# Stick-breaking attention: transposes by query tile into a step buffer, a float32 value product one step later, and one elementwise product on GpSimd

## The chip, the cores and the metric

The kernel runs on one core of a Trainium2 chip. The metric is device time in microseconds (us) of one execution; lower is better. The kernel before has a median of 3163.7 us over three runs.

The engines are called as in the profile: PE (matrix products; PEld is its weight load), DVE (VectorE), ACT (ScalarE), POOL (GpSimd) and SP (which issues nearly all DMAs).

## What is computed

One layer of a hybrid block over 2048 tokens of width 1024, all in float32. The part that the change touches is branch B, stick-breaking attention with 16 heads of 64 values, strictly causal:

```python
logits = einsum('bqhd,bkhd->bhqk', q, k) * 64 ** -0.5
log_fail = where(ki < qi, log_sigmoid(-logits), 0)
between = cumsum(log_fail, axis=3, reverse=True) - log_fail
w = where(ki < qi, exp(log_sigmoid(logits) + between), 0)
out = einsum('bhqk,bkhd->bqhd', w, v)
```

So the weight of a key is its sigmoid ("stick weight") times the product, over all later keys up to the query, of one minus theirs ("running product"). Around it stand an RMS norm, one large input projection, a Mamba-2 scan (branch A, 16 heads), gates, two branch projections and an output projection.

## The kernel before

Activations are kept with features on the partitions. Large products run in the type `float32r`, with both operands split in a high and a low half, so that one product of 128 x 128 x 512 is three PE instructions (`product`, L139). The stages follow each other: norm and transposes of the input, the first projections, V (`prep_v`, `unit_v`, L389 to L423), the scan of branch A with its projections (`ssd`, up to L640), attention with the rest of the projections as fill, and the final projections.

V is made by 16 units per group of four heads. A unit sums 24 products into `vps`; ACT rounds the result to its high half, DVE subtracts to get the low half (L421, L422), and SP stores both, side by side, to `vst` in memory.

Attention works in 160 steps `(h, qs, kc)`: for each head, query blocks `qs` of 512 from the last to the first, and for each of them key blocks `kc` of 512 from the diagonal back to the first. So each head has ten steps, four of them diagonal (`kc == qs`) and six full. A query block has four query tiles `i` of 128.

- `attn_load` (from L809) loads Q, K and V of a step two steps ahead.
- `attn_qk(s, i)` (from L829) makes the logits of one query tile in two PE products, `lg`. ACT makes both sigmoids, `tc` (of the negative, L843) and `sw` (the stick weight, L845). On diagonal steps POOL masks both with a select (L847, L849) and only the columns up to the diagonal are used. DVE runs the running product along the keys, from the end (L852), with the carry of the later key block as start; DVE multiplies `sw` by it (L853); POOL copies the carry `cy` for the next key block (L856). POOL also sets the one start column of `tc` (L842).
- `attn_tr(s, kb)` (from L862) transposes on PE, for one key tile `kb`, the blocks of all four query tiles into `wtp`; ACT rounds them to `wh` (L870) and DVE subtracts to get `wl` (L872).
- `attn_av(s, kb)` (from L875) adds two products to `po`: stationary is V with its high and low halves, 128 columns, moving are `wh` and then `wl`. At the last key block ACT and DVE add the two halves of `po` and gate them with `zl` (L886 to L893).

The order of PE is fixed: a helper chains every PE instruction to the one traced before it. The other engines get their instructions from a scheduler that mostly follows the traced order. In one step, query tile by query tile, PE does the transposes of key tile `i`, the logits of the next step's tile `i`, the value product of key tile `i - 2`, and some fill; after the four tiles come the last two value products and fill. The fill is a stream of 34 x 96 projection products for nine tenths of the steps, and 192 products of the first output projection for the last head; `FW` (L27) sets the share of each of the six fill places of a step.

Of the kernel before, what the change touches and what calls it, by code (L numbers as in the profile page):

```python
# [18 lines left out]
P = 128  # L19
# [4 lines left out]
HD = 64  # L24
EPS = 1e-6
WARM = 24
FW = (0.8, 0.9, 1.0, 1.0, 1.1, 1.2)  # L27

COL_Z = 0
COL_X = 1024  # L30
# [18 lines left out]
def hybrid_kernel(ctx, tc, x, norm_pre, w_in, b_gate, conv_w, conv_b, dt_bias, a_log, d_skip,  # L49
# [57 lines left out]

    kst = [drp.tile([P, L], F32, name=f"kst{h}") for h in range(HEADS)]
    qst = [drp.tile([P, L], F32, name=f"qst{h}") for h in range(HEADS)]
    vst = [drp.tile([L, 4, P], F32, name=f"vst{i}") for i in range(HEADS // 4)]  # L110
    csd = drp.tile([HEADS, L], F32, name="csd")
    ytd = [drp.tile([D, TB], F32, name=f"ytd{t}") for t in range(NTB)]
    otd = [drp.tile([D, TB], F32, name=f"otd{t}") for t in range(NTB)]
# [272 lines left out]
    with tc.tile_pool(name="va", bufs=2) as va, tc.tile_pool(name="vp", bufs=2, space=PSUM) as vp:  # L386
        kn = va.tile([P, NCH, 16], F32, name="kn", bufs=1)

        def prep_v(i):  # L389
            c0, cw = vch[i]  # L390
            vh, vl = [], []
            for k in range(KT):
                raw = va.tile([P, cw], F32, name="vraw", tag="vraw", bufs=4)
                nc.sync.dma_start(raw, w_in[k * P:(k + 1) * P, c0:c0 + cw])
                h = va.tile([P, cw], F32R, name="vhi", tag="vhi", bufs=12)
                nc.scalar.copy(h, raw)
                l = va.tile([P, cw], F32R, name="vlo", tag="vlo", bufs=12)
                nc.vector.tensor_sub(l, raw, h.bitcast(F32))
                vh.append(h)
                vl.append(l)  # L400
            return vh, vl

        def unit_v(i, c, wv):
            c0, cw = vch[i]
            vh, vl = wv
            off = cw - VW
            tb, o = c // CPB, (c % CPB) * P
            ps = vp.tile([P, TB], F32, name="vps", tag="vps", bufs=3)
            for k in range(KT):
                xh, xl = hh[tb][:, k, o:o + P], hl[tb][:, k, o:o + P]  # L410
                matmul(ps[:, :cw], xh, vh[k], start=(k == 0), stop=False)
                yield
                matmul(ps[:, :cw], xh, vl[k], start=False, stop=False)
                yield
                matmul(ps[:, :cw], xl, vh[k], start=False, stop=(k == KT - 1))
                yield
            if off:
                nc.vector.tensor_copy(kn[:, c, :], ps[:, :16])
            v = va.tile([P, 4, 2, HD], F32R, name="vt", tag="vt", bufs=3)
            src = ps[:, off:cw].rearrange("p (h d) -> p h d", d=HD)  # L420
            nc.scalar.copy(v[:, :, 0, :], src)  # L421
            nc.vector.tensor_sub(v[:, :, 1, :], src, v[:, :, 0, :].bitcast(F32))  # L422
            nc.sync.dma_start(vst[i][c * P:(c + 1) * P], v.bitcast(F32).rearrange("p h s d -> p h (s d)"))  # L423

        def last_k():
            knf = kn.rearrange("p c d -> p (c d)")
            kd = kst[HEADS - 1].rearrange("(s d) t -> d s t", s=2)
            for r0 in range(0, NCH * 16, P):
                n = min(P, NCH * 16 - r0)
                tp = vp.tile([P, P], F32, name="ktp", tag="ktp")  # L430
                transpose(tp[:n], knf[:, r0:r0 + n], ident)
                kt = va.tile([P, 2, P], F32R, name="kt", tag="kt")
                nc.scalar.copy(kt[:n, 0, :], tp[:n])
                nc.vector.tensor_sub(kt[:n, 1, :], tp[:n], kt[:n, 0, :].bitcast(F32))
                for c in range(n // 16):
                    t0 = (r0 // 16 + c) * P
                    nc.sync.dma_start(kd[HD - 16:HD, :, t0:t0 + P], kt[c * 16:(c + 1) * 16].bitcast(F32))

        wv = prep_v(0)
        for tb in range(NTB):  # L440
            run(proj(w9, tb, done_qk(ev, 9, tb)))
        for i in range(len(vch)):
            for c in range(NCH):
                if c == max(0, NCH - 6) and i + 1 < len(vch):
                    nxt = prep_v(i + 1)
                run(unit_v(i, c, wv))
            if i == 0:
                later(20, last_k)
            if i + 1 < len(vch):
                wv = nxt  # L450
        wb = prep_a(COL_B)
        flush()
# [326 lines left out]

    steps = [(h, qs, kc) for h in range(HEADS) for qs in reversed(range(NTB)) for kc in reversed(range(qs + 1))]  # L780
    last_head = min(i for i, s in enumerate(steps) if s[0] == HEADS - 1)
    fills = {"gen": fill_h(), "left": n_main, "pos": 6 * last_head, "acc": 0.0, "late": False}

    def tick():
        clock[0] += 1
# [3 lines left out]
    def fill(i):  # L789
        f = fills  # L790
        if f["pos"] <= 0:
            for _ in f["gen"]:
                tick()
            if f["late"]:
                return
            f.update(gen=fill_y(box_y), left=8 * 24, pos=6 * (len(steps) - last_head) - 3, acc=0.0, late=True)
        f["acc"] += f["left"] / f["pos"] * FW[i]
        f["pos"] -= 1
        while f["acc"] >= 1.0:
            f["acc"] -= 1.0  # L800
            f["left"] -= 1
            if next(f["gen"], 0) == 0:
                f["left"] = 0
                break
            tick()
# [3 lines left out]
    def attn_load(s):  # L809
        if s >= len(steps):  # L810
            return
        h, qs, kc = steps[s]
        if (h, qs) not in qts:
            qa = ab.tile([P, TB], F32R, name="qa", tag="qa", bufs=2)
            qb = ab.tile([P, TB], F32R, name="qb", tag="qb", bufs=2)
            cols = slice(qs * TB, (qs + 1) * TB)
            nc.sync.dma_start(qa.bitcast(F32), qst[h][:, cols])
            nc.sync.dma_start(qb[0:HD].bitcast(F32), qst[h][HD:P, cols])
            nc.sync.dma_start(qb[HD:P].bitcast(F32), qst[h][0:HD, cols])
            qts[h, qs] = qa, qb  # L820
        if (h, kc) not in kts:
            k = ab.tile([P, TB], F32R, name="kt", tag="kt", bufs=4)
            nc.sync.dma_start(k.bitcast(F32), kst[h][:, kc * TB:(kc + 1) * TB])
            v = ab.tile([P, CPB, P], F32R, name="vt", tag="vt", bufs=4)
            nc.sync.dma_start(v.bitcast(F32), vst[h // 4][kc * TB:(kc + 1) * TB, h % 4, :].rearrange(
                "(c p) d -> p c d", p=P))
            kts[h, kc], vts[h, kc] = k, v

    def attn_qk(s, i):  # L829
# [20 lines left out]
                                    pattern=[[-1, P]], channel_multiplier=1)  # L850
        tr = t[:, W::-1]
        nc.vector.tensor_tensor_scan(tr, tr, tr, 1.0 if diag else carry[h, qs, i], ALU.mult, ALU.min)  # L852
        nc.vector.tensor_mul(w[:, :W], w[:, :W], t[:, 1:W + 1])  # L853
        if kc > 0:
            c = ab.tile([P, 1], F32, name="cy", tag="cy", bufs=8)
            nc.gpsimd.tensor_copy(c, t[:, 0:1])  # L856
# [2 lines left out]

    wts = {}  # L860

    def attn_tr(s, kb):  # L862
        h, qs, kc = steps[s]
        q0 = kb if kc == qs else 0
        lo = q0 * P
        tp = ap.tile([P, TB], F32, name="wtp", tag="wtp", bufs=3)
        for i in range(q0, CPB):
            transpose(tp[:, i * P:(i + 1) * P], ws[s, i][:, kb * P:(kb + 1) * P], ident)
        wh = ab.tile([P, TB], F32R, name="wh", tag="wh", bufs=3)
        nc.scalar.copy(wh[:, lo:], tp[:, lo:])  # L870
        wl = ab.tile([P, TB], F32R, name="wl", tag="wl", bufs=3)
        nc.vector.tensor_sub(wl[:, lo:], tp[:, lo:], wh[:, lo:].bitcast(F32))  # L872
        wts[s, kb] = lo, wh, wl

    def attn_av(s, kb):  # L875
        h, qs, kc = steps[s]
        lo, wh, wl = wts.pop((s, kb))
        if (h, qs) not in pos:
            pos[h, qs] = ap.tile([P, TB], F32, name="po", tag="po", bufs=1)
        po, v = pos[h, qs], vts[h, kc]  # L880
        first = kc == qs and kb == 0
        final = kc == 0 and kb == CPB - 1
        matmul(po[:, lo:], v[:, kb, :], wh[:, lo:], start=first, stop=False, skip_group_check=True)
        matmul(po[:, lo:], v[:, kb, :], wl[:, lo:], start=False, stop=final, skip_group_check=True)
        if final:
            e0 = (h % 2) * HD  # L886
            mine, other = slice(e0, e0 + HD), slice(HD - e0, P - e0)
            z = ab.tile([P, TB], F32, name="zl", tag="zl", bufs=1)
            nc.sync.dma_start(z[mine], zsd[qs][h * HD:(h + 1) * HD, :])
            o = gz.tile([P, TB], F32, name="o", tag="gz", bufs=2)  # L890
            nc.scalar.copy(o[mine], po[other])
            nc.vector.tensor_add(o[mine], o[mine], po[mine])  # L892
            nc.vector.tensor_mul(o[mine], o[mine], z[mine])  # L893
            nc.sync.dma_start(otd[qs][h * HD:(h + 1) * HD, :], o[mine])
# [9 lines left out]
    for s in range(len(steps)):  # L904
        attn_load(s + 2)
        for i in range(CPB):
            attn_tr(s, i)
            attn_qk(s + 1, i)
            if i >= 2:
                attn_av(s, i - 2)  # L910
            fill(i)
        for i in range(2, CPB):
            attn_av(s, i)
            fill(i + 2)
    for _ in fills["gen"]:
        pass
    close_ap()
# [150 lines left out]
```

## Time and profile before

| what | value |
|---|---|
| median of three runs | 3163.7 us (3163.27 to 3165.02) |
| span of the profiled execution | 3163.6 us |
| PE busy | 3024.1 us, 96% of the span |
| DVE busy | 2457.2 us, 78% |
| ACT busy | 1585.7 us, 50% |
| POOL busy | 477.9 us, 15% |
| attention loop, first transpose to end | 935.6 to 2663.4 us |
| chain that ended last | PE 53%, DVE 33% of the span |

The profiled execution has no other time of its own than this span. A group's row gives the line, engine, operation, tiles (written <- read) and shape, the count, then the busy time and the mean of one, then the idle time of the engine just before them and what ended it. A timeline's row gives the start and the time until the end of the merged group in us. PE instructions are pipelined, so the distance between two starts is shorter than one instruction's time. A float32 product leaves two records on PE. A busy DVE or POOL may be waiting inside an instruction.

### The profile page before, as it was taken

Reading aid. Unit: us, or ns where it says so; the run is one execution under the profiler, and the core shown is the slowest. Engines: PE = TensorE matmul, PEld = TensorE weight load, DVE = VectorE, ACT = ScalarE, POOL = GpSimd, SP = SyncE. Lnnn points to the kernel's source line nnn. Section 1 sums busy time; section 2 is a strip of 40 time slices with the busy share of each in tenths; the row PEclk is TensorE's granted clock in tenths of the full one; section 3 lists DMA queues with packets and bytes.
Section 4 is the critical chain, followed back from the end, with each engine's and each line's share of the span. In section 5 each row is a group of like instructions: output and inputs, shape, how many; then the busy total and the mean of one; then the engine's idle time right before and its main releaser. Section 6 shows DMA issues by size and latency. Waiting matters only on the chain.

```text
span 3163.6 us, 48155 instructions
## 1 busy us (share of the span) xinstructions
PE 3024.1 (96%) x16169; PEld 2496.9 (79%) x16169; DVE 2457.2 (78%) x4357; ACT 1585.7 (50%) x3102; POOL 477.9 (15%) x1626
## 2 busy tenths in 40 slices
PE   8999999999999999999999999999999989999998
PEld 6899888787877777777777777777777767888887
DVE  7321688768869989989899999989998899756553
ACT  6211345434446666566565666566665656333321
POOL 0000011100111212122212121222111231101000
PEclk9999999999999999999999999999999999999999
DMA  5532022212243334224323333334233334555452
GB/s 165 148 122 93 24 71 80 68 40 67 72 128 89 90 89 110 80 81 113 93 70 103 94 97 91 87 94 114 69 89 90 111 117 144 176 148 167 133 167 70
DMA packets 298816, 320.63 MB, mean 101 GB/s; under 512 B 23148, under 2 KB 187848, under 8 KB 298568
## 3 DMA queue, kind: packets, MB, share of 16 engines
q1 hardware_dynamic: 298416, 317.51, 34.6%
q8 instruction: 128, 2.10, 0.3%
q14 instruction: 120, 0.98, 0.1%
q10 hardware_dynamic: 152, 0.05, 0.0%
HBM read 216.67 MB, written 100.79 MB: 100 GB/s over the span
## 4 chain that ended last, share of the span: by engine, by line
PE 53%; DVE 33%; issue 5%; DMA 4%; ACT 4%; POOL 1%; SPq 0%; DVEq 0%; POOLq 0%; ACTq 0%
PE proj L74 30%; DVE tc L852 13%; PE po L74 8%; DVE sw L853 7%; PE vps L74 6%; DVE wl L872 5%; PE wtp L77 4%; PE lg L74 3%; DMA csb<-csd 2%; ACT sw L845 1%; ACT wh L870 1%; PE yp L74 1%; DVE acc L474 1%; DVE o L893 1%; DVE o L892 1%
## 5 line engine op out<-in xcount | busy, mean ns | idle before, releaser
L74 PE MATMUL proj<-hh,whi 128*128 128x512 f32 x1920 | 762.0, 397 | 0.1
L74 PE MATMUL proj<-hh,wlo 128*128 128x512 f32 x1920 | 761.7, 397 | 0.0
L74 PE MATMUL proj<-hl,whi 128*128 128x512 f32 x1920 | 760.4, 396 | 1.3 <-DVE hl L286 1.1
L870 ACT CAST wh<-wtp 128x512 fp32r<-128x512 f32 (+3 forms) x640 | 337.1, 527 | 390.2 <-PE wtp L77 386.6
L852 DVE TENSOR_TENSOR_SCAN tc<-tc,cy 128x513 f32<-128x513 f32 x384 | 490.9, 1278 | 0.3 <-ACT tc L843 0.3
L872 DVE TENSOR_TENSOR wl<-wtp,wh 128x512 fp32r<-128x512 f32 (+3 forms) x640 | 383.0, 599 | 81.5 <-ACT wh L870 80.3
L77 PE MATMUL wtp<-ident,sw 128*128 128x128 f32 x2176 | 369.9, 277 | 72.2 <-DVE sw L853 70.1
L853 DVE TENSOR_TENSOR sw<-sw,tc 128x512 f32<-128x512 f32 (+3 forms) x640 | 394.2, 616 | 50.5 <-POOL sw L849 13.5
L77 PEld LDWEIGHTS wtp<-ident,sw 128*128 128x128 f32 x2176 | 280.7, 141 | 181.0 <-DVE sw L853 99.1
L74 PEld LDWEIGHTS proj<-hl,whi 128*128 128x128 f32 x1920 | 362.6, 189 | 72.6 <-DVE hl L286 2.5
L74 PEld LDWEIGHTS proj<-hh,wlo 128*128 128x128 f32 x1920 | 362.6, 189 | 70.7 <-issue 0.3
L74 PEld LDWEIGHTS proj<-hh,whi 128*128 128x128 f32 x1920 | 362.7, 189 | 70.1 <-ACT hh L285 0.5
L845 ACT ACTIVATE sw<-lg 128x512 f32<-128x512 f32 (+3 forms) x640 | 346.1, 541 | 49.8 <-PE wtp L77 49.6
L843 ACT ACTIVATE tc<-lg 128x512 f32<-128x512 f32 (+3 forms) x640 | 349.1, 545 | 18.7 <-PE lg L74 13.1
L132 ACT CAST whi<-wraw 128x512 fp32r<-128x512 f32 x248 | 154.3, 624 | 280.5 <-PE proj L74 178.9
L74 PE MATMUL lg<-kt,qa 128*128 128x512 f32 (+3 forms) x640 | 285.1, 445 | 0.0
L74 PE MATMUL po<-wl,vt 128*128 128x512 f32 (+3 forms) x640 | 242.6, 379 | 29.0 <-DVE wl L872 28.2
L852 DVE TENSOR_TENSOR_SCAN tc<-tc 128x129 f32<-128x129 f32 (+3 forms) x256 | 218.1, 852 | 26.3 <-POOL tc L847 25.2
L74 PE MATMUL lg<-kt,qb 128*128 128x512 f32 (+3 forms) x640 | 234.6, 367 | 0.0
L74 PE MATMUL po<-wh,vt 128*128 128x512 f32 (+3 forms) x640 | 232.4, 363 | 0.0
L134 DVE TENSOR_TENSOR wlo<-wraw,whi 128x512 fp32r<-128x512 f32 x246 | 173.4, 706 | 73.3 <-ACT whi L132 70.5
L856 POOL COPY cy<-tc 128x1 f32<-128x1 f32 x384 | 133.6, 348 | 448.7 <-DVE tc L852 448.7
(202 smaller groups left out, 4887.8 us busy)
## 6 DMA issues: line engine op xcount, KB each, us to landing
wraw<-in_w_in SPq DMA_DIRECT2D x120, 256.0 KB, 3.0
vst<-vt SPq DMA_DIRECT2D x64, 256.0 KB, 2.0
csb<-csd SPq DMA_DIRECT2D x64, 256.0 KB, 4.4
qa<-qst SPq DMA_DIRECT2D x64, 256.0 KB, 3.5
qb<-qst SPq DMA_DIRECT2D x128, 128.0 KB, 3.8
kt<-kst SPq DMA_DIRECT2D x64, 256.0 KB, 3.2
vt<-vst SPq DMA_DIRECT2D x64, 256.0 KB, 3.0
gtd<-zb SPq DMA_DIRECT2D x64, 256.0 KB, 2.1
```

The lines of the kernel that those rows point to most:

```text
L74: chain(nc.tensor.matmul(*a, **k))
L77: chain(nc.tensor.transpose(*a))
L132: nc.scalar.copy(h, raw)
L134: (eng or nc.vector).tensor_tensor(l, raw, h.bitcast(F32), op=ALU.subtract)
L474: nc.vector.scalar_tensor_tensor(acc, xp[:, i:i + TB], pv[:, col:col + 1], acc, op0=ALU.mult, op1=ALU.add)
L843: nc.scalar.activation(t[:, :W], lg[:, :W], AF.Sigmoid, scale=-0.125)
L845: nc.scalar.activation(w[:, :W], lg[:, :W], AF.Sigmoid, scale=0.125)
L852: nc.vector.tensor_tensor_scan(tr, tr, tr, 1.0 if diag else carry[h, qs, i], ALU.mult, ALU.min)
L853: nc.vector.tensor_mul(w[:, :W], w[:, :W], t[:, 1:W + 1])
L856: nc.gpsimd.tensor_copy(c, t[:, 0:1])
L870: nc.scalar.copy(wh[:, lo:], tp[:, lo:])
L872: nc.vector.tensor_sub(wl[:, lo:], tp[:, lo:], wh[:, lo:].bitcast(F32))
```

## The change

- `attn_tr(s, i)` now takes a query tile: it transposes the tile's blocks for all key tiles into `wtp`, and ACT copies them, in float32, into a buffer `wt` of the whole step with key tile and query as its free dimensions. `wl` and the rounding are gone. On diagonal steps only the blocks up to the diagonal are transposed, and POOL clears one block of `wt`.
- `attn_av(s)` makes the value product of a whole step in four float32 products. V is 64 columns wide; even key tiles go to partitions 0 to 63 of `po`, odd ones to 64 to 127, and the halves are added at the end as before. It is called after the second query tile of the next step.
- The product of `sw` and the running product (L853) goes to POOL.
- V is stored once, in float32, with the partition as the first dimension of `vst`, so that a unit's store has runs of 256 bytes and a load runs of 1 KB.
- `FW` has five fill places per step.

```diff
-FW = (0.8, 0.9, 1.0, 1.0, 1.1, 1.2)
+FW = (1.0, 1.0, 1.2, 1.2, 0.6)
...
-    vst = [drp.tile([L, 4, P], F32, name=f"vst{i}") for i in range(HEADS // 4)]
+    vst = [drp.tile([P, 4, NCH, HD], F32, name=f"vst{i}") for i in range(HEADS // 4)]
...
-            v = va.tile([P, 4, 2, HD], F32R, name="vt", tag="vt", bufs=3)
-            src = ps[:, off:cw].rearrange("p (h d) -> p h d", d=HD)
-            nc.scalar.copy(v[:, :, 0, :], src)
-            nc.vector.tensor_sub(v[:, :, 1, :], src, v[:, :, 0, :].bitcast(F32))
-            nc.sync.dma_start(vst[i][c * P:(c + 1) * P], v.bitcast(F32).rearrange("p h s d -> p h (s d)"))
+            v = va.tile([P, 4, HD], F32, name="vt", tag="vt", bufs=3)
+            nc.scalar.copy(v, ps[:, off:cw].rearrange("p (h d) -> p h d", d=HD))
+            nc.sync.dma_start(vst[i][:, :, c, :], v)
...
-            v = ab.tile([P, CPB, P], F32R, name="vt", tag="vt", bufs=4)
-            nc.sync.dma_start(v.bitcast(F32), vst[h // 4][kc * TB:(kc + 1) * TB, h % 4, :].rearrange(
-                "(c p) d -> p c d", p=P))
+            v = ab.tile([P, CPB, HD], F32, name="vt", tag="vt", bufs=4)
+            nc.sync.dma_start(v, vst[h // 4][:, h % 4, kc * CPB:(kc + 1) * CPB, :])
...
-        nc.vector.tensor_mul(w[:, :W], w[:, :W], t[:, 1:W + 1])
+        nc.gpsimd.tensor_tensor(w[:, :W], w[:, :W], t[:, 1:W + 1], op=ALU.mult)
...
-    def attn_tr(s, kb):
+    def attn_tr(s, i):
         h, qs, kc = steps[s]
-        q0 = kb if kc == qs else 0
-        lo = q0 * P
+        n = i + 1 if kc == qs else CPB
         tp = ap.tile([P, TB], F32, name="wtp", tag="wtp", bufs=3)
-        for i in range(q0, CPB):
-            transpose(tp[:, i * P:(i + 1) * P], ws[s, i][:, kb * P:(kb + 1) * P], ident)
-        wh = ab.tile([P, TB], F32R, name="wh", tag="wh", bufs=3)
-        nc.scalar.copy(wh[:, lo:], tp[:, lo:])
-        wl = ab.tile([P, TB], F32R, name="wl", tag="wl", bufs=3)
-        nc.vector.tensor_sub(wl[:, lo:], tp[:, lo:], wh[:, lo:].bitcast(F32))
-        wts[s, kb] = lo, wh, wl
+        sw = ws.pop((s, i))
+        for kb in range(n):
+            transpose(tp[:, kb * P:(kb + 1) * P], sw[:, kb * P:(kb + 1) * P], ident)
+        if i == 0:
+            wts[s] = ab.tile([P, CPB, TB], F32, name="wt", tag="wt", bufs=2)
+            if kc == qs:
+                nc.gpsimd.memset(wts[s][:, 1, 0:P], 0.0)
+        nc.scalar.copy(wts[s][:, 0:n, i * P:(i + 1) * P], tp[:, 0:n * P].rearrange("p (k q) -> p k q", q=P))
...
-        matmul(po[:, lo:], v[:, kb, :], wh[:, lo:], start=first, stop=False, skip_group_check=True)
-        matmul(po[:, lo:], v[:, kb, :], wl[:, lo:], start=False, stop=final, skip_group_check=True)
-        if final:
+        wt = wts.pop(s)
+        for kb in range(CPB):
+            lo = kb * P if kc == qs and kb > 1 else 0
+            e = (kb % 2) * HD
+            matmul(po[e:e + HD, lo:], v[:, kb, :], wt[:, kb, lo:], start=(kc == qs and kb < 2),
+                   stop=(kc == 0 and kb >= 2), skip_group_check=True)
+        if kc == 0:
...
             attn_tr(s, i)
             attn_qk(s + 1, i)
-            if i >= 2:
-                attn_av(s, i - 2)
             fill(i)
-        for i in range(2, CPB):
-            attn_av(s, i)
-            fill(i + 2)
+            if i == 1 and s > 0:
+                attn_av(s - 1)
+                fill(CPB)
+    attn_av(len(steps) - 1)
```

## Rows read from the trace of the kernel before

**Rows 1.** Attention loop: stretch, length; busy PE, PEld, DVE, ACT, POOL; clock, DMA

```profile
935.60:2663.40 1727.80, 1621.66 (x8216) 1303.44 (x8214) 1575.11 (x2248) 1059.35 (x2225) 379.57 (x1537) 0.99 0.33 94
```

**Rows 2.** Loop groups: count | busy us, mean ns | idle us, releaser

```profile
L852 DVE TENSOR_TENSOR_SCAN tc<-tc,cy 128x513 f32<-128x513 f32 x384 | 490.9, 1278 | 0.3 <-ACT tc L843 0.3
...
L853 DVE TENSOR_TENSOR sw<-sw,tc 128x512 f32<-128x512 f32 (+1 forms) x638 | 393.5, 617 | 50.3 <-POOL sw L849 13.5 <-ACT tc L843 0.5
L872 DVE TENSOR_TENSOR wl<-wtp,wh 128x512 fp32r<-128x512 f32 (+3 forms) x640 | 383.0, 599 | 81.5 <-ACT wh L870 80.3
L77 PE MATMUL wtp<-ident,sw 128*128 128x128 f32 x2176 | 369.9, 277 | 72.2 <-DVE sw L853 70.1 <-DMA qb<-qst 1.0 <-DMA qst<-hlt 0.3
...
L74 PE MATMUL po<-wl,vt 128*128 128x512 f32 (+1 forms) x639 | 242.3, 379 | 29.0 <-DVE wl L872 28.2
...
L852 DVE TENSOR_TENSOR_SCAN tc<-tc 128x513 f32<-128x513 f32 x253 | 215.8, 853 | 9.6 <-POOL tc L847 8.5
```

**Rows 3.** Loop groups, same columns: POOL and further DVE instructions

```profile
L856 POOL COPY cy<-tc 128x1 f32<-128x1 f32 x381 | 133.0, 349 | 446.8 <-DVE tc L852 446.8
...
L849 POOL TENSOR_SCALAR_AFFINE_SELECT sw<-sw 128x128 f32<-128x128 f32 x253 | 92.1, 364 | 13.8 <-ACT sw L845 12.8
L847 POOL TENSOR_SCALAR_AFFINE_SELECT tc<-tc 128x128 f32<-128x128 f32 x253 | 78.6, 311 | 91.3 <-ACT tc L843 88.7
...
L134 DVE TENSOR_TENSOR wlo<-wraw,whi 128x512 fp32r<-128x512 f32 x84 | 58.7, 699 | 0.0
...
L893 DVE TENSOR_TENSOR o<-o,zl 64x512 f32<-64x512 f32 x63 | 44.2, 701 | 2.0
```

**Rows 4.** PE in order of time, loop: start us, duration us, line, tiles

```profile
1508.40 0.60 PE L77 MATMUL wtp<-ident,sw 128*128 128x128 f32 x4
1508.76 0.48 PE L74 MATMUL lg<-kt,qa 128*128 128x512 f32 x1
1509.07 0.39 PE L74 MATMUL lg<-kt,qb 128*128 128x512 f32 x1
1509.30 0.40 PE L74 MATMUL po<-wh,vt 128*128 128x512 f32 x1
1509.54 0.40 PE L74 MATMUL po<-wl,vt 128*128 128x512 f32 x1
```

**Rows 5.** PE in order of time, scan stage, products 64 columns wide

```profile
395.74 0.39 PE L74 MATMUL proj<-hl,whi 128*128 128x512 f32 x1
396.06 0.44 PE L74 MATMUL yp<-dl,xd 128*64 128x128 f32 x4
...
397.64 0.39 PE L74 MATMUL yp<-csb,S 128*64 128x128 f32 x4
397.96 0.33 PE L77 MATMUL xnp<-ident,xT 128*128 128x128 f32 x1
```

**Rows 6.** PE in order of time, scan stage, products 128 columns wide

```profile
388.92 0.39 PE L74 MATMUL proj<-hh,wlo 128*128 128x512 f32 x1
389.15 1.05 PE L74 MATMUL stp<-xe,bn 128*128 128x128 f32 x8
389.96 0.48 PE L74 MATMUL proj<-hh,whi 128*128 128x512 f32 x1
```

**Rows 7.** DVE in order of time near the end of the attention loop

```profile
2511.61 1.28 DVE L852 TENSOR_TENSOR_SCAN tc<-tc,cy 128x513 f32<-128x513 f32 x1
2512.99 1.50 DVE L853 TENSOR_TENSOR sw<-sw,tc 128x512 f32<-128x512 f32 x1
...
2514.62 2.09 DVE L852 TENSOR_TENSOR_SCAN tc<-tc,cy 128x513 f32<-128x513 f32 x1
```

**Rows 8.** POOL in order of time, the same stretch

```profile
2511.92 2.02 POOL L695 TENSOR_TENSOR mp<-mp 128x512 f32<-128x512 f32 x1
2513.91 1.72 POOL L695 TENSOR_TENSOR scr<-scr 128x512 f32<-128x512 f32 x1
...
2518.43 1.27 POOL L695 TENSOR_TENSOR mp<-mp 128x512 f32<-128x512 f32 x1
```

More of the change, by code (lines that the diff above doesn't have):

```diff
@@ L781, in hybrid_kernel @@
     last_head = min(i for i, s in enumerate(steps) if s[0] == HEADS - 1)
-    fills = {"gen": fill_h(), "left": n_main, "pos": 6 * last_head, "acc": 0.0, "late": False}
+    fills = {"gen": fill_h(), "left": n_main, "pos": len(FW) * last_head, "acc": 0.0, "late": False}
     def tick():
@@ L795, in fill @@
                 return
-            f.update(gen=fill_y(box_y), left=8 * 24, pos=6 * (len(steps) - last_head) - 3, acc=0.0, late=True)
+            f.update(gen=fill_y(box_y), left=8 * 24, pos=len(FW) * (len(steps) - last_head) - 3, acc=0.0, late=True)
         f["acc"] += f["left"] / f["pos"] * FW[i]
@@ L860, in hybrid_kernel, with attn_av @@
     wts = {}
-    def attn_tr(s, kb):
+    def attn_tr(s, i):
         h, qs, kc = steps[s]
-        q0 = kb if kc == qs else 0
-        lo = q0 * P
+        n = i + 1 if kc == qs else CPB
         tp = ap.tile([P, TB], F32, name="wtp", tag="wtp", bufs=3)
-        for i in range(q0, CPB):
-            transpose(tp[:, i * P:(i + 1) * P], ws[s, i][:, kb * P:(kb + 1) * P], ident)
-        wh = ab.tile([P, TB], F32R, name="wh", tag="wh", bufs=3)
-        nc.scalar.copy(wh[:, lo:], tp[:, lo:])
-        wl = ab.tile([P, TB], F32R, name="wl", tag="wl", bufs=3)
-        nc.vector.tensor_sub(wl[:, lo:], tp[:, lo:], wh[:, lo:].bitcast(F32))
-        wts[s, kb] = lo, wh, wl
-    def attn_av(s, kb):
+        sw = ws.pop((s, i))
[6 more added lines that the diff above has]
+        nc.scalar.copy(wts[s][:, 0:n, i * P:(i + 1) * P], tp[:, 0:n * P].rearrange("p (k q) -> p k q", q=P))
+    def attn_av(s):
         h, qs, kc = steps[s]
-        lo, wh, wl = wts.pop((s, kb))
         if (h, qs) not in pos:
@@ L880, in attn_av @@
         po, v = pos[h, qs], vts[h, kc]
-        first = kc == qs and kb == 0
-        final = kc == 0 and kb == CPB - 1
-        matmul(po[:, lo:], v[:, kb, :], wh[:, lo:], start=first, stop=False, skip_group_check=True)
-        matmul(po[:, lo:], v[:, kb, :], wl[:, lo:], start=False, stop=final, skip_group_check=True)
-        if final:
+        wt = wts.pop(s)
[5 more added lines that the diff above has]
+        if kc == 0:
             e0 = (h % 2) * HD
```

## The prediction

> **What bounds the kernel now.** I read the page's shares first, then the windows, then the groups of the attention loop, then timelines. The page shows PE busy nearly everywhere and DVE close behind in the middle; the change lies in the middle, so the window over the attention loop comes next. It lasts 1727.8 us, with PE busy for 1621.7 and DVE for 1575.1 [rows 1]. There are 160 steps: 64 diagonal ones (four per head, where the key block is the query block) and 96 full ones. A mean step is 10.8 us.
>
> Busy PE time holds pipeline tails, so I count PE by the distance from start to start. In a full step, one query tile costs 0.36 us for four transposes, 0.31 + 0.23 = 0.54 for the logits, and a pair of value products 0.48 [rows 4]; a fill product of the projections goes out every 0.23 us [rows 6]. The code plans 3456 fill products (34 x 96 + 192), 21.6 a step, 4.97 us. A full step is then 4 x (0.36 + 0.54 + 0.48) + 4.97 = 10.49 us. A diagonal step has 10 of 16 blocks: 0.9 + 0.625 x 4 x (0.54 + 0.48) + 4.97 = 8.42. Together 96 x 10.49 + 64 x 8.42 = 1546 us. So PE loses 1727.8 - 1546 = 182 us to waits. The groups name 101 us of them: transposes stand idle 72.2 us, nearly all for the product `sw` on DVE, and the second value product 29.0 us for the split `wl` on DVE [rows 2]. Both engines are nearly full, and tightly tied: the first transpose of a step needs the last `sw` of the step before.
>
> **The change, part by part.**
>
> Removed from DVE: `wl`, 383.0 us, and `sw`, 393.5 us [rows 2], half of its work in the loop. The 64 subtractions on `vt` go too, in a stage where PE runs without a gap: worth nothing.
>
> The value product on PE. Four float32 products 64 columns wide replace eight of 128 columns. The scan stage has that form: `yp` alternates between the two halves of the output partitions. A float32 product leaves two records. From 396.06 to 397.64 there are 28 records in 1.58 us, 0.056 us each; `stp`, 128 columns wide with as many moving columns, takes 0.81 us for 8, or 0.101 each [rows 5, 6]. So the halves run side by side. No row has 512 moving columns in float32, so I scale by 4: 0.226 us a record, 8 records in a full step 1.81 us (side by side) or 3.23 (one after the other). I take the first, since `yp` has the same halves and types. Around `yp` the distances are 0.32 us on both sides instead of 0.23 [rows 5]: a switch costs 0.09 each way, 0.18 a step. Full step: 1.99 against 4 x 0.48 = 1.92, +0.07. Diagonal step: two products of 512 together 0.90, 256 beside 128 0.45, switches 0.18, so 1.53 against 0.625 x 1.92 = 1.20: +0.33. Sum 96 x 0.07 + 64 x 0.33 = 28 us, rounded to 30. PE then needs 1576 us.
>
> The waits on PE. The tile `sw` is now used a whole step after its logits, tile by tile, and the value product a step after its transposes. The chain from logits to finished `sw` has some 10 us where it had as little as one tile's. If just the 101 named us go, the loop takes 1728 - 101 + 30 = 1657.
>
> The product on POOL. 640 products of 278,528 columns in all are worth 544 of 512 columns. POOL's two-input add of that size takes 1.27 us when undisturbed [rows 8]: 691 us, on an engine now busy for 380 [rows 1]. That fits, but POOL does not run freely beside DVE. The add at 2511.92 ends at 2513.94, 1.05 us after the running scan; the DVE product that then wants to start ends 0.55 later, at 2514.49; the next add ends at 2515.63, 1.14 after that; the next scan needs 2.09 us and ends 1.08 after the add [rows 7, 8]. They take turns, with an overlap of some 0.2 us. So I count what cannot overlap: scan and product 1.08 + 1.10 = 2.18 us a pair, 544 x 2.18 = 1186; `wlo` and the gating of `o`, 147 x 0.55 = 81; POOL's selects 92.1 + 78.6; carry copies between 0 and 133 [rows 3]. Together 1438 to 1571, about 1500, under PE's 1576. In front of the product nothing new waits: the scan does as before. Behind it on POOL stand the carry copy, needed a step later, and on diagonal steps the selects of the next tile.
>
> ScalarE: the same 640 evictions, without rounding, into a tile that three dimensions address; the loop has it busy for 1059 of 1728 us [rows 1]. Nothing, unless copies came out half as long again (+170 us, still hidden).
>
> DMA and SP: the value store halves its bytes but cuts runs to 256 B; three buffers and the 24 products of a unit cover it, and a late store could only hold up a stage in which PE waits for nothing today. The loads halve their bytes, with longer runs. Counts on SP stay. The memset per diagonal step (64) is off every chain. The end: the last value product follows the loop; 1 to 2 us, inside the rounding. The new fill weights move the same 3456 products.
>
> The sum: before, the loop was 10% above its fuller engine (1575). After, 1576 on PE and 1500 on the shared memory path are as close, but with a step of slack; I take 5%, 79 us: 1655, which the 1657 above confirms. The ends are 1576 (no waits: 3012 in all) and 1576 + 182 = 1758 (the waits stay: 3194). The profiled execution's span is 3163.6 and the median 3163.7, so nothing lies around it. 3163.6 - 1727.8 + 1655 = 3091.
>
> **The rivals.**
>
> *DVE and POOL exclude each other fully.* Mechanism: scan and product never overlap, and all POOL work that reads the operands waits as well. By whole records: scans 490.9 + 215.8, products 691, `wlo` and `o` 103, selects and copies 304 [rows 2, 3, 8]: 1805 us, 3241 in all, slower. For it: the scan of 2.09 us. Against it: the 0.2 us of overlap at each hand-over [rows 7, 8]. It decides once a pair costs (1728 - 81 - 171 - 70) / 544 = 2.58 us instead of 2.18. The Trainium skill's rule in "SBUF — State Buffer", SBUF: two separate sides, is this rival: a DVE instruction with two SBUF inputs and a GpSimd one that reads SBUF take an exclusive lock for the whole instruction. The trace agrees that one waits for the other, not that all of it is lost. 0.14.
>
> *The line on POOL decides the diagonal steps.* POOL works in order, and there the next scan needs its select, which stands behind product and copy. Per diagonal step: 0.625 x 4 x (1.28 + 1.27), copies and memsets 1.6, selects 2.7: 10.7 us, against 8.7 on PE, 64 x 2.0 = 128 us more than 1576, less some 10 that full steps take back: 1694 plus a few waits, 1700 to 1735, 3136 to 3171. For it: the carry copy already stands idle 446.8 us for the scan [rows 3]. Against it: a full step gives slack on both sides. 0.13.
>
> *The halves don't run side by side,* so the change doesn't do what it says: 8 x 0.101 x 4 = 3.23 us a full step, +1.42, diagonal +0.9: 194 us, 3285. Rows 5 speak against it. 0.04.
>
> *Other waits take the place,* ScalarE's evictions or the late head's sums on POOL: 3194. 0.07.
>
> **How the numbers follow.** The forecast has 0.62, with 3030 to 3150 as its own range. A measurement of this kernel tells 0.2%, 6.3 us, from no change. Faster: 0.62, and 0.07 of the line on POOL: 0.69. Same: 0.05 of it. Slower: 0.14 + 0.04 + 0.07 and 0.01: 0.26. The range runs from near the waitless end to past the fourth rival: 3030 to 3205; beyond it lie the two slow rivals, 0.18.
>
> **What would show it.** Right: a loop near 1655 us; `po` in pairs of records some 0.45 us apart; idle time before `wtp` nearly gone; DVE busy for some 800 us plus its waits for POOL; scan records stretched past 1.28 us, up to 2.1. Wrong: `po` records 0.4 us apart without partners; scans and products that fill the loop end to end (first rival); POOL selects waiting behind products while PE stands before a transpose (second).

## The result, and the profile after

The changed kernel takes 3065.5 us (median of four runs, 3064.8 to 3068.7), against 3163.6 us for the kernel before on the same chip: a ratio of 0.969, 95% interval 0.968 to 0.970. That is 98 us less, inside the range, 25 us below the forecast of 3091.

The page of the changed kernel first: the shares of the engines, and the chain of work that ended last.

```profile
PE 3017.0 (98%) x16169; PEld 2344.7 (76%) x16169; DVE 1893.6 (62%) x3013; ACT 1589.1 (52%) x3102; POOL 1318.0 (43%) x2330
...
PE 90%; DVE 5%; DMA 2%; POOL 1%; issue 1%; ACT 1%; SPq 0%; POOLq 0%; ACTq 0%; DVEq 0%
```

PE now makes up 90% of the chain, where it had 53%, and DVE 5% where it had 33%. The windows of the changed kernel, before, in and after the attention loop (columns as in rows 1), show where the time came from:

```profile
0.00:934.60 934.60, 912.21 (x5745) 787.11 (x5746) 556.35 (x1395) 369.26 (x588) 58.81 (x60) 0.99 0.29 80
934.60:2567.50 1632.90, 1614.57 (x8218) 1150.44 (x8215) 1040.60 (x971) 1062.90 (x2225) 1217.79 (x2239) 0.99 0.34 94
2567.50:3067.00 499.50, 490.23 (x2209) 407.13 (x2208) 296.69 (x647) 156.98 (x290) 41.41 (x31) 1.00 0.48 149
```

The loop fell from 1727.8 us [rows 1] to 1632.9; the other two stretches together got 1.7 us shorter. DVE is busy for 1041 us in the loop instead of 1575, POOL for 1218 instead of 380. The groups of the loop that answer to [rows 2] and [rows 3]:

```profile
L850 POOL TENSOR_TENSOR sw<-sw,tc 128x512 f32<-128x512 f32 (+1 forms) x638 | 734.9, 1152 | 332.2 <-DVE tc L849 238.7 <-ACT wt L870 49.1 <-ACT tc L840 19.4
L849 DVE TENSOR_TENSOR_SCAN tc<-tc,cy 128x513 f32<-128x513 f32 x384 | 589.6, 1545 | 173.3 <-ACT tc L840 134.4 <-POOL tc L839 16.5 <-POOL sw L850 13.3
...
L77 PE MATMUL wtp<-ident,sw 128*128 128x128 f32 x2176 | 342.1, 272 | 1.2 <-POOL sw L850 1.1
...
L74 PE MATMUL po<-wt,vt 128*64 128x512 f32 (+2 forms) x1280 | 284.3, 555 | 3.0 <-ACT wt L870 3.0
...
L853 POOL COPY cy<-tc 128x1 f32<-128x1 f32 x382 | 235.0, 615 | 0.0
...
L849 DVE TENSOR_TENSOR_SCAN tc<-tc 128x513 f32<-128x513 f32 x253 | 222.5, 879 | 369.9 <-POOL tc L844 352.1 <-POOL tc L839 17.7
...
L846 POOL TENSOR_SCALAR_AFFINE_SELECT sw<-sw 128x128 f32<-128x128 f32 x253 | 108.8, 430 | 4.0 <-ACT sw L842 0.2
...
L844 POOL TENSOR_SCALAR_AFFINE_SELECT tc<-tc 128x128 f32<-128x128 f32 x253 | 75.6, 299 | 39.1 <-ACT tc L840 38.1 <-ACT wt L870 0.3 <-issue 0.3
L134 DVE TENSOR_TENSOR wlo<-wraw,whi 128x512 fp32r<-128x512 f32 x85 | 73.6, 867 | 5.7 <-PE wtp L77 2.2 <-ACT whi L132 1.4 <-PE proj L74 0.7
...
L891 DVE TENSOR_TENSOR o<-o,zl 64x512 f32<-64x512 f32 x63 | 61.4, 975 | 2.3 <-DMA zl<-zsd 0.3
```

`wl` is gone and the product runs on POOL. What one instruction takes has grown for DVE instructions with two SBUF operands and for two of POOL's: the scan from 1278 to 1545 ns, `wlo` from 699 to 867, `o` from 701 to 975, POOL's carry copy from 349 to 615 and its select on `sw` from 364 to 430; its select on `tc` has not, 311 and 299 [rows 2, 3]. And the idle time of PE before a transpose, 72.2 us [rows 2], is 1.2 us. The waits in the loop, longest in total first (engine, line, awaited; us in total, times, longest), confirm it:

```profile
DVE tc L849 <- POOL tc L844: 352.1, 237, 5.0
POOL sw L850 <- DVE tc L849: 238.7, 257, 2.6
...
PE sps L74 <- DVE scr L708: 5.4, 1, 5.4
PE proj L74 <- DVE mp L719: 4.8, 1, 4.8
...
PE lg L74 <- ACT sw L842: 3.3, 3, 1.6
PE po L74 <- ACT wt L870: 3.0, 2, 2.3
```

DVE and POOL wait for each other by the hundred microseconds, and PE's named waits are few, the long ones near the end of the loop: together 16.5 us in these four rows. PE in order of time around one value product of a full step, to be laid beside [rows 4]:

```profile
1510.52 0.40 PE L74 MATMUL proj<-hh,whi 128*128 128x512 f32 x1
1510.84 1.94 PE L74 MATMUL po<-wt,vt 128*64 128x512 f32 x8
1512.71 0.50 PE L74 MATMUL proj<-hl,whi 128*128 128x512 f32 x1
1513.05 0.39 PE L74 MATMUL proj<-hh,wlo 128*128 128x512 f32 x1
```

From 1510.84 to 1512.71 there are eight records in 1.87 us; before and behind it stand 0.32 and 0.34 us where fill products are 0.23 apart. On a diagonal step the logits are narrower; those of a tile 256 columns wide:

```profile
1499.41 0.36 PE L74 MATMUL lg<-kt,qa 128*128 128x256 f32 x1
1499.61 0.28 PE L74 MATMUL lg<-kt,qb 128*128 128x256 f32 x1
1499.73 0.40 PE L74 MATMUL proj<-hh,wlo 128*128 128x512 f32 x1
```

They take 0.32 us, where half of the 0.54 us of 512 columns is 0.27. DVE and then POOL around the value product above, to be laid beside [rows 7, 8]:

```profile
1508.06 1.29 DVE L849 TENSOR_TENSOR_SCAN tc<-tc 128x513 f32<-128x513 f32 x1 [1.66 <-POOL tc L844]
1509.27 0.66 DVE L134 TENSOR_TENSOR wlo<-wraw,whi 128x512 fp32r<-128x512 f32 x1
1509.85 2.11 DVE L849 TENSOR_TENSOR_SCAN tc<-tc,cy 128x513 f32<-128x513 f32 x1
```

```profile
1509.49 1.39 POOL L850 TENSOR_TENSOR sw<-sw,tc 128x512 f32<-128x512 f32 x1 [1.23 <-DVE tc L849]
1510.82 1.12 POOL L853 COPY cy<-tc 128x1 f32<-128x1 f32 x1
```

The scan at 1509.85 takes 2.11 us because POOL's product runs until 1510.88, and ends 1.08 us after it; the carry copy, 0.19 us in the median of its 384, then waits inside its record for the scan, 1.12 us.

### The profile page after: what moved, and what is told of

It reads as the page before. It is cut to its first block, busy times and chain, and to the rows that moved or that the text cites. A ratio compares the mean times of both kernels' runs of the same rounds, so it can differ in the third digit from the quotient of the medians.

```text
span 3067.0 us, 47628 instructions
## 1 busy us (share of the span) xinstructions
PE 3017.0 (98%) x16169; PEld 2344.7 (76%) x16169; DVE 1893.6 (62%) x3013; ACT 1589.1 (52%) x3102; POOL 1318.0 (43%) x2330
## 4 chain that ended last, share of the span: by engine, by line
PE 90%; DVE 5%; DMA 2%; POOL 1%; issue 1%; ACT 1%; SPq 0%; POOLq 0%; ACTq 0%; DVEq 0%
PE proj L74 50%; PE po L74 14%; PE lg L74 8%; PE wtp L77 7%; PE vps L74 6%; DMA csb<-csd 2%; PE yp L74 1%; DVE acc L472 1%; PE stp L74 1%; DVE tc L849 1%; DVE S L538 1%; DVE dl L514 0%; POOL sw L850 0%; DVE csb L520 0%; DVE dl L518 0%
## 5 line engine op out<-in xcount | busy, mean ns | idle before, releaser
L850 POOL TENSOR_TENSOR sw<-sw,tc 128x512 f32<-128x512 f32 (+3 forms) x640 | 736.3, 1150 | 333.3 <-DVE tc L849 239.8
L849 DVE TENSOR_TENSOR_SCAN tc<-tc,cy 128x513 f32<-128x513 f32 x384 | 589.6, 1545 | 173.3 <-ACT tc L840 134.4
L870 ACT COPY wt<-wtp 128x512 f32<-128x512 f32 (+3 forms) x640 | 336.2, 526 | 397.0 <-PE wtp L77 376.2
L849 DVE TENSOR_TENSOR_SCAN tc<-tc 128x129 f32<-128x129 f32 (+3 forms) x256 | 224.8, 878 | 388.1 <-POOL tc L844 370.3
L504 POOL TENSOR_TENSOR xe<-xd,dec 128x512 f32<-128x512 f32 x32 | 50.4, 1576 | 831.0 <-DVE xd L502 831.0
L77 PE MATMUL wtp<-ident,sw 128*128 128x128 f32 x2176 | 342.1, 272 | 1.2 <-POOL sw L850 1.1
L74 PE MATMUL po<-wt,vt 128*64 128x512 f32 (+2 forms) x1280 | 284.3, 555 | 3.0 <-ACT wt L870 3.0
L853 POOL COPY cy<-tc 128x1 f32<-128x1 f32 x384 | 235.3, 613 | 0.0
L134 DVE TENSOR_TENSOR wlo<-wraw,whi 128x512 fp32r<-128x512 f32 x246 | 186.9, 761 | 74.2 <-ACT whi L132 69.4
L74 PEld LDWEIGHTS po<-wt,vt 128*64 128x64 f32 x1280 | 77.9, 136 | 153.2 <-issue 144.1
```

The source lines that it names most:

```text
L74: chain(nc.tensor.matmul(*a, **k))
L77: chain(nc.tensor.transpose(*a))
L134: (eng or nc.vector).tensor_tensor(l, raw, h.bitcast(F32), op=ALU.subtract)
L504: nc.gpsimd.tensor_tensor(heads(xe), heads(xd), tok(dec), op=ALU.mult)
L850: nc.gpsimd.tensor_tensor(w[:, :W], w[:, :W], t[:, 1:W + 1], op=ALU.mult)
L870: nc.scalar.copy(wts[s][:, 0:n, i * P:(i + 1) * P], tp[:, 0:n * P].rearrange("p (k q) -> p k q", q=P))
```

## The experiments

The theory was slack: the gain comes from using each `sw` a step later, and PE is the bound now. The first rival was relief: it comes from the 777 us taken off DVE. Unless said otherwise the edits are made to the changed kernel, and ratios are against the kernel before.

### The product back on DVE (e1)

```diff
-        nc.gpsimd.tensor_tensor(w[:, :W], w[:, :W], t[:, 1:W + 1], op=ALU.mult)
+        nc.vector.tensor_mul(w[:, :W], w[:, :W], t[:, 1:W + 1])
```

> The changed kernel with the product of stick weight and running product back on DVE. Theory (slack: the gain comes from using each sw tile a whole step later, and PE is the bound now): DVE gets some 390 us back, 1300 of the loop's 1633, and the port is relieved; PE still has no wait; 3050 to 3075. Rival (relief: the gain comes from the 777 us taken off DVE): half of the relief is undone, about half of the 98 us is lost: 3100 to 3125.

Measured: 3057.5 us, ratio 0.966 (0.965 to 0.968). Groups of the whole run:

```profile
L849 DVE TENSOR_TENSOR_SCAN tc<-tc,cy 128x513 f32<-128x513 f32 x384 | 491.9, 1281 | 56.1 <-ACT tc L840 52.4 <-POOL tc L839 2.1
L850 DVE TENSOR_TENSOR sw<-sw,tc 128x512 f32<-128x512 f32 (+3 forms) x640 | 400.8, 626 | 74.7 <-POOL cy L853 1.4
...
L77 PE MATMUL wtp<-ident,sw 128*128 128x128 f32 x2176 | 342.0, 272 | 0.0
```

DVE has the 401 us again, the scans are back at 1.28 us, and PE waits for nothing before a transpose. So the move to POOL is no part of the gain. This version was 8 us faster than the changed kernel, though from another set of runs, and their intervals touch.

### The product on POOL in the kernel before (e2)

```diff
-        nc.vector.tensor_mul(w[:, :W], w[:, :W], t[:, 1:W + 1])
+        nc.gpsimd.tensor_tensor(w[:, :W], w[:, :W], t[:, 1:W + 1], op=ALU.mult)
```

> The kernel before with one part of the change alone: the product of stick weight and running product on POOL. Theory (slack): the last sw of a step, which the first transposes wait for, comes 0.6 us or more later than from DVE, so 0.3 to 0.8 us a step are lost: 3210 to 3290. Rival (relief of DVE): 394 us less on DVE help at once: 3060 to 3130.

Measured: 3258.2 us, ratio 1.029 (1.027 to 1.031). The waits:

```profile
PE wtp L77 <- POOL sw L853: 146.1, 168, 3.2
```

This half of the relief, without slack, costs 94 us: in the old order PE waits for the product, 146 us instead of 70 [rows 2], and the product got later. It is no clean test of less work on DVE, as the product's move made it later by itself; and the granted clock of the profiled execution is 0.984 instead of 0.993, so a part of the 94 us is slower work behind the waits (more on this with e5).

### Transposes by key tile (e5)

```diff
-        sw = ws.pop((s, i))
-        for kb in range(n):
-            transpose(tp[:, kb * P:(kb + 1) * P], sw[:, kb * P:(kb + 1) * P], ident)
+        q0 = i if kc == qs else 0
+        for q in range(q0, CPB):
+            transpose(tp[:, q * P:(q + 1) * P], ws[s, q][:, i * P:(i + 1) * P], ident)
...
-        nc.scalar.copy(wts[s][:, 0:n, i * P:(i + 1) * P], tp[:, 0:n * P].rearrange("p (k q) -> p k q", q=P))
+        nc.scalar.copy(wts[s][:, i, q0 * P:], tp[:, q0 * P:])
```

> The changed kernel with the transposes by key tile again, so that the first transposes of a step need the sw of all four query tiles of the step before; step buffer, float32 value product one step later and product on POOL stay. Theory (slack): idle time before wtp comes back, 50 to 130 us, and the time is 3115 to 3190. Rival (relief of DVE): DVE has the same work as in the changed kernel, 3060 to 3075.

Measured: 3693.4 us, ratio 1.167 (1.165 to 1.169): the sign of the theory, but far outside its numbers. PE's longest wait, the window of the loop (columns as in rows 1), and PE in order of time behind one wait:

```profile
PE wtp L77 <- POOL sw L850: 387.6, 207, 5.1
```

```profile
935.90:3195.00 2259.10, 1854.30 (x8229) 1292.85 (x8228) 974.78 (x973) 1077.58 (x2226) 974.82 (x2239) 0.90 0.24 68
```

```profile
1499.57 0.47 PE L77 MATMUL wtp<-ident,sw 128*128 128x128 f32 x1 [3.10 <-POOL sw L850]
...
1500.70 0.63 PE L74 MATMUL proj<-hh,whi 128*128 128x512 f32 x1
1501.12 0.63 PE L74 MATMUL proj<-hl,whi 128*128 128x512 f32 x1
```

PE waits where the theory said. The size is my error: this edit leaves only the fill of one query tile, about 1.2 us (a share of 1.2 in 5.0 of 3456 fill products in 160 steps, 0.24 us each), between the last logits of a step and the next step's first transposes; in the kernel before three value products and three shares of fill stood there, 4.4 us in the median. And the waits are only a part of the 628 us. PE's granted clock is 0.90 in this loop instead of 0.99: behind the wait of 3.10 us, from 1499.6 to 1505.4 us, it is 0.50, the lower of its two levels (1.2 GHz), and fill products stand 0.42 us apart instead of 0.23. PE is busy for 1854 us with the same work that took 1615, so some 240 of the 628 us are slower work, and PE's idle time, 405 us where it was 18, makes up the rest. The next run puts PE work back in between.

### Key tiles, DVE's product, and PE work in between (e12)

```diff
-FW = (1.0, 1.0, 1.2, 1.2, 0.6)
+FW = (0.75, 0.75, 0.8, 0.9, 1.8)
...
-            if i == 1 and s > 0:
+            if i == 3 and s > 0:
                 attn_av(s - 1)
                 fill(CPB)
```

together with the edits of e1 and e5.

> The float32 value product one step later, but transposes by key tile and the product of the weights on DVE as in the kernel before; fill shares 0.75, 0.75, 0.8, 0.9, 1.8 and the value product behind the last query tile, so that as much PE work stands between the last logits of a step and the next step's first transposes as in the kernel before. Theory (the tie of the first transposes to the last sw costs by itself): idle time before wtp as before, some 70 us or more, 3095 to 3160. Rival (without the low half on DVE the last sw is ready in time, the tie is harmless): 3050 to 3075.

Measured: 3090.1 us, ratio 0.977 (0.975 to 0.978): 5 us below the theory's range and 15 above the rival's. The waits:

```profile
PE wtp L77 <- DVE sw L850: 20.8, 25, 2.3
```

Transposes again wait for `sw`, but for 21 us on PE where it was 70 [rows 2]. So the tie of the first transposes to the last `sw` costs about 33 us here (e12 against e1), and 74 us of the gain are there without removing it. The two runs differ in fill shares and in the place of the value product too, so the 33 is not the tie's alone. Nor does this run favour slack alone: the tie stands as in the kernel before, the PE work between last logits and first transposes is 4.9 us where it was 4.6 (means in the two traces), and yet 49 us of the wait for `sw` are gone, with `wl` off DVE. How much of that is relief of DVE and how much the 0.3 us was not tried separately.

### The value product at the end of its own step (e4)

```diff
-            if i == 1 and s > 0:
-                attn_av(s - 1)
-                fill(CPB)
-    attn_av(len(steps) - 1)
+        attn_av(s)
+        fill(CPB)
```

> The changed kernel with the value product at the end of its own step, behind the fill of the last query tile, instead of after the second tile of the next step. Theory (slack on the transposes is what counts, the delay of the value product is secondary): PE waits for the last eviction of a step by 0 to 0.25 us, 3065 to 3105. Rival (the delay of the value product is as important): over 0.4 us a step, 3130 or more.

Measured: 3062.5 us, ratio 0.968 (0.966 to 0.969). With one eviction on ScalarE between transposes and product, the fill of one tile is delay enough.

### The old form of the value product, early and later (e8, e10)

```diff
-        nc.scalar.copy(wts[s][:, 0:n, i * P:(i + 1) * P], tp[:, 0:n * P].rearrange("p (k q) -> p k q", q=P))
+        hi, lw = (x[:, 0:n, i * P:(i + 1) * P] for x in wts[s])
+        tv = tp[:, 0:n * P].rearrange("p (k q) -> p k q", q=P)
+        nc.scalar.copy(hi, tv)
+        nc.vector.tensor_tensor(lw, tv, hi.bitcast(F32), op=ALU.subtract)
...
+            matmul(po[:, lo:], v[:, kb, :], wt[:, kb, lo:], start=(kc == qs and kb == 0), stop=False,
+                   skip_group_check=True)
+            matmul(po[:, lo:], v[:, kb, :], wu[:, kb, lo:], start=False, stop=(kc == 0 and kb == CPB - 1),
+                   skip_group_check=True)
```

with V split and stored as in the kernel before and one copy of each step buffer. In e8 the value product stands as in e4; in e10 it follows the first query tile of the next step (`if i == 0 and s > 0`).

> As the run before it (value product at the end of its own step, transposes by query tile, product on POOL), but the value product in the old form: rounding to a high half on ScalarE, subtraction for the low half on DVE (383 us back on DVE), eight products of 128 columns, V stored in two halves; the two step buffers have one copy each, for want of memory. Theory (slack): PE has 28 us less work by the prediction's count and nothing else changes: within 35 us of the run before it, 3040 to 3100. Rival (relief of DVE): half of the gain goes, 3110 or more.

Measured, e8: 3145.0 us, ratio 0.994 (0.993 to 0.996). This was the rival's number, 82 us above e4.

```profile
PE po L74 <- DVE wu L875: 80.2, 86, 3.0
```

But DVE is not full here (busy for 1374 of the loop's 1703 us); the waits are for the last `wu` of a step, which in the steps looked at stands on DVE behind a scan of 1.7 to 2.0 us that takes turns with POOL. If its lateness is the cause, one tile of delay must cure it:

> The float32r form of the value product again (rounding, subtraction on DVE, eight products), by query tile and with the product of the weights on POOL, but the value product stands one query tile later than in the run before of this form: behind the first tile's work of the next step, some 2.5 us. Theory (there the subtraction of the last tile came too late for PE, the form itself costs nothing): most of the 217 us of waits of PE and its weight load for the low half go, 3045 to 3090. Rival (the load on DVE, or the form, costs it): 3120 to 3150 as before.

Measured, e10: 3059.7 us, ratio 0.967 (0.966 to 0.969).

```profile
PE po L74 <- DVE wu L875: 22.3, 26, 2.9
```

It does: 85 us for a place one query tile later in PE's order, with the same work on every engine. So the float32 form is not what pays either; the old form, given slack, is as fast, and its PE work is even less (busy for 1579 us of the loop instead of 1615). What the float32 form does is shorten the chain in front of the product by one DVE instruction; that it needs less delay for this reason is an inference from e4 and e8.

### Side by side or not (e3, e9)

```diff
-        for kb in range(CPB):
+        for kb in (0, 2, 1, 3):
```

> The changed kernel with the four float32 products of a step in the order of key tiles 0, 2, 1, 3, so that two to the lower half of the columns are followed by two to the upper half. Theory (the halves run side by side because neighbours alternate): on a full step only one pair of records in the middle can overlap, some 3.0 us instead of 1.87 us, and the time is 3150 to 3240. Rival (PE looks far enough ahead to overlap them in any order, or they never overlapped): 3060 to 3075.

Measured, e3: 3066.6 us, ratio 0.969 (0.967 to 0.970): no difference. A full step's product (PE in order of time) still takes 1.87 us:

```profile
1509.48 1.94 PE L74 MATMUL po<-wt,vt 128*64 128x512 f32 x8
1511.35 0.50 PE L74 MATMUL proj<-hl,whi 128*128 128x512 f32 x1
```

Either the order does not matter, or the halves never overlapped. To tell these apart, all four products go to one half:

```diff
-            e = (kb % 2) * HD
+            e = (h % 2) * HD
...
-            nc.scalar.copy(o[mine], po[other])
-            nc.vector.tensor_add(o[mine], o[mine], po[mine])
+            nc.scalar.copy(o[mine], po[mine])
```

> The changed kernel with all four float32 products of a step in one half of the output partitions (that of the head), so that none has a neighbour in the other half; the addition of the two halves at the end of a block falls away. Theory (the halves run side by side, in whatever order the four stand): a full step takes 8 x 0.43 = 3.44 us instead of 1.87, a diagonal one 2.37 instead of 1.43, 96 x 1.57 + 64 x 0.94 = 211 us more: 3240 to 3290. Rival (a record of 512 columns in float32 costs what it costs, alone or beside another): 3055 to 3075.

Measured, e9: 3288.7 us, ratio 1.039 (1.038 to 1.041). PE in order of time, a full and a diagonal step:

```profile
1475.06 3.65 PE L74 MATMUL po<-wt,vt 128*64 128x512 f32 x8
1478.64 0.50 PE L74 MATMUL proj<-hh,wlo 128*128 128x512 f32 x1
...
1508.70 2.58 PE L74 MATMUL po<-wt,vt 128*64 128x512 f32 x8
1511.21 0.50 PE L74 MATMUL proj<-hl,whi 128*128 128x512 f32 x1
```

3.58 us instead of 1.87 for a full step, 2.51 instead of 1.43 for a diagonal one. By these, 96 x 1.71 + 64 x 1.08 = 233 us were to be expected over the changed kernel, and 223 were measured. The halves do run side by side, and by e3 they do so even when the partner in the other half is issued two products later.

### What DVE and POOL share (e6, e7)

Two additions of 640 DVE instructions into a buffer that nothing reads, alike in number and width: one reads two operands in SBUF, the other one in PSUM and one in SBUF.

```diff
+        x = ab.tile([P, TB], F32, name="xx", tag="xx", bufs=1)
+        nc.vector.tensor_mul(x[:, :W], t[:, 0:W], t[:, 1:W + 1])
```

```diff
+        x = ab.tile([P, TB], F32, name="xx", tag="xx", bufs=1)
+        nc.vector.tensor_tensor(x[:, 0:n * P], tp[:, 0:n * P], sw[:, 0:n * P], op=ALU.subtract)
```

> The changed kernel with one more DVE instruction per tile, a product of two SBUF operands (the running product with itself, one column apart) into a buffer that nothing reads; 640 of them, 0.6 us each at full width. Theory (DVE instructions with two SBUF inputs and POOL's product take turns): 544 x 0.55 = 300 us more on what they share, 1500 + 300 = 1800 against PE's 1613: 3200 to 3300. Rival (they share nothing that matters; only DVE's own time counts, 1041 + 330 us of 1633): 3060 to 3080.

> The changed kernel with one more DVE instruction per tile, as many and as wide as in the run before it, but with one operand in PSUM (the transposed tile) and one in SBUF, into a buffer that nothing reads: the work of the removed wl. Theory (turns are taken only over two SBUF operands): DVE gets 383 us, still under PE's 1613; 3060 to 3090. Rival (DVE's time is what counts, whatever the operands): as the run before it, within 30 us.

Measured: e6 3282.2 us, ratio 1.037 (1.035 to 1.039); e7 3078.8 us, ratio 0.973 (0.971 to 0.974). Groups of e6, then of e7:

```profile
L850 POOL TENSOR_TENSOR sw<-sw,tc 128x512 f32<-128x512 f32 (+3 forms) x640 | 829.6, 1296 | 467.3 <-DVE tc L849 373.1 <-ACT sw L842 33.3 <-ACT tc L840 12.8
...
L849 DVE TENSOR_TENSOR_SCAN tc<-tc,cy 128x513 f32<-128x513 f32 x384 | 710.2, 1849 | 0.9
L852 DVE TENSOR_TENSOR xx<-tc 128x512 f32<-128x512 f32 (+3 forms) x640 | 403.7, 631 | 21.3
...
L77 PE MATMUL wtp<-ident,sw 128*128 128x128 f32 x2176 | 359.4, 281 | 135.7 <-POOL sw L850 133.4
```

```profile
L850 POOL TENSOR_TENSOR sw<-sw,tc 128x512 f32<-128x512 f32 (+3 forms) x640 | 712.5, 1113 | 361.6 <-DVE tc L849 266.6 <-ACT tc L840 20.9 <-ACT wt L870 20.8
L849 DVE TENSOR_TENSOR_SCAN tc<-tc,cy 128x513 f32<-128x513 f32 x384 | 610.4, 1590 | 1.0 <-ACT tc L840 0.6
L872 DVE TENSOR_TENSOR xx<-wtp,sw 128x512 f32<-128x512 f32 (+3 forms) x640 | 377.9, 591 | 71.0 <-ACT wt L870 59.2 <-POOL sw L850 6.4 <-POOL tc L839 2.2
...
L77 PE MATMUL wtp<-ident,sw 128*128 128x128 f32 x2176 | 342.8, 273 | 9.6 <-POOL sw L850 5.8 <-DVE xx L872 3.6
```

The same 380 to 400 us on DVE cost 217 us with two SBUF operands and 13 with one. In e6 a scan takes 1.85 us in the mean, POOL's product 1.30, and PE waits 136 us for `sw`; in e7 PE hardly waits. The Trainium skill, "SBUF — State Buffer", SBUF: two separate sides, states that a DVE instruction with two SBUF inputs takes an exclusive lock against a GpSimd one that reads SBUF; the 217 and 13 us agree. The two additions also stand at different places, behind the scan and behind the transposes; what the place does was not tried separately.

### Two variations together (e11)

The edits of e1 and e4.

> The changed kernel with two variations that were each a little faster or equal: the product of the weights back on DVE, and the value product at the end of its own step. Theory (PE is the bound, a step of delay is more than the value product needs, POOL's product only crowds DVE): 3045 to 3062. Rival (DVE's product makes the last tile late for the earlier value product): 3062 to 3090.

Measured: 3057.5 us, ratio 0.966 (0.965 to 0.968): as e1. With PE the bound there is nothing left for the second variation to give. e1, e10 and e11, at 3057.5 to 3059.7 us, are the fastest of the study.

## Why the prediction was right

**The waits on PE go.** Right, and more fully than forecast. The two named waits, 101 us [rows 2], became 1.2 and 3.0. I had kept 79 us of stall, as 5% over the fuller engine; PE's four waits above sum to 16.5. This term of the sum was too large by some 60 us. The gain stays with either half of the relief taken back (e1, e10).

**The count of PE's work.** 1576 us, against 1632.9 - 16.5 = 1616 us that PE did not spend on those waits: too small by 40. The trace shows where most of it lies. The value product: 0.09 + 1.87 + 0.11 = 2.07 us a full step where 1.99 was reckoned, 0.09 + 1.43 + 0.11 = 1.63 a diagonal one where it was 1.53; 14 us in all, for the first fill product behind it is late as well. The logits of a diagonal step: scaled by columns to 1.35 us, in the trace 1.56 over the four widths; 13 us, as narrow products cost more than their share. The clock: in three stretches near the end of the loop, 20 us in all, each behind one of PE's waits (5.40, 4.84 and 2.29 us), the granted clock is 0.50, and fill products stand 0.43 us apart instead of 0.23; by this 9 us, an estimate. The fill itself was counted right, 0.231 us in the median. The 1546 us of the kernel before are scaled in the same way, so its 182 us of waits were too many.

The two errors, 60 us too much stall and 40 us too little work, have opposite signs and leave the 22 us by which the loop, 1633 against 1655, came out shorter. That they nearly cancel is luck: with the stall alone put right, the forecast would have been some 3030 us.

**The value product side by side, and scaled from 128 to 512 columns.** Right, 1.87 against 1.81 us before the switches, and shown by e9. The switch costs 0.09 to 0.11 on either side. The Trainium skill, "TensorEngine Tiling (Array Packing)", Key Properties, says both, that tiles run in parallel and that a change of mode drains the engine; these rows agree.

**The product on POOL under PE's bound.** Right in that PE does not wait for it. The 1500 us of the shared path were not measured by themselves; e6, which adds some 300 to them by the same count, has a loop of 1847 us and PE in waits, which fits. The turn-taking shows in the changed kernel as I read it in [rows 7, 8]: 1.08 us for a scan behind a product. But I counted the move as a part of the relief, and it is not one: e1 without it is as fast or faster, e2 with it alone is slower.

**What the removal of `wl` is worth.** I wrote that the idle time named after `wl` and `sw` would go, and it did. Once there is slack, the place of the value product behind its operands decides, not DVE's time: e7 gives DVE 378 us back for 13 us, e8 and e10 give it the real subtraction and lose 82 us or nothing, by the place alone. In the old order that is not shown: no run takes `wl` alone off the kernel before, and e12 leaves room for it. Nor does any run put `wl` and the product back on DVE together.

**The rivals.** Full exclusion of DVE and POOL: the scans did stretch, to 1.55 us in the mean, yet a pair keeps its overlap. The line on POOL: the scan waits 352 us for POOL's select, as that rival said, but with a step of slack PE waits for `sw` in only one place, 1.1 us. One half at a time: refuted by e9. Other waits: not found.

## What to carry to other kernels

Before work is moved off a full engine, look at what the bound engine waits for: here two waits came from operands made just before their use, and with one step (or even one tile) of distance in the issue order neither half of the 777 us taken off the producer was needed for the gain (e1, e10). An elementwise instruction moved from DVE to GpSimd is not off DVE's hands if both read two operands in SBUF: count the two together, by what they take in turns. When PE's work is counted, read narrow products in rows of their own width instead of scaling, and count what a switch costs on both sides. When a change makes PE wait, look at its granted clock too: in e5 some 240 of 628 us were slower work.

## What was not expected

The order of the four products does not matter: e3 puts neighbours in the same half, and the step still takes 1.87 us. Short GpSimd instructions suffer most from the turns: the carry copy of one column takes 0.62 us in the mean, against 0.35 [rows 3], as it stands behind whole scans. And e5 shows how steep the price of a missing distance is: with transposes tied to the last `sw`, and with 1.2 us of PE work in between, 628 us, 3.9 us in each of 160 steps, more than a third of it at the lower clock. How much of it POOL's product brings about and how much the missing fill was not tried separately.
